# The decayed keys of the HGRN heads: turned by TensorE, or by VectorE blocks and a trip through memory

## The chip, the core and the metric

The kernel runs on one core of a Trainium2 chip. A core has five engines with an instruction stream each: TensorE (PE in the profile, its weight loads PEld), VectorE (DVE), ScalarE (ACT), GpSimd (POOL) and SyncE (SP). Each runs its own stream strictly in order; semaphores hold an instruction back until what it needs has been done elsewhere. The metric is the device time of one execution in microseconds, lower is better.

## The reference, cut to what matters

One layer of a diffusion backbone on 256 latent tokens and 256 context tokens, model width 2048. After a norm, one projection feeds a convolution branch and a bidirectional gated linear recurrence (HGRN) with 8 heads of 128 channels; both are merged, projected, and followed by an MLP. The part in question is the recurrence. For each head, with keys `k = 1 - f` and gates `f` out of a sigmoid:

```python
def hgrn_final_state(k, v, logf):
    a = jnp.cumsum(logf, axis=1)
    return jnp.einsum('blhk,blhv->bhkv', k * jnp.exp(a[:, -1:] - a), v)
...
s_f = hgrn_final_state(kc_f, vc, lfc_f)
s_b = hgrn_final_state(jnp.flip(kc_b, 1), jnp.flip(vc, 1), jnp.flip(lfc_b, 1))
...
o, _, _ = hgrn_bidir(q_prep(p_q), to_heads(p_i.astype(f32)), hgrn_forget(p_ff, lb_f),
                     hgrn_forget(p_fb, lb_b), s_f, s_b)
```

The state of a head is a sum over the 256 context tokens of (decayed key) times (value), in both directions: two matrices of 128 by 128. The latent tokens then read that state and each other.

## The kernel before, in words

Weights stream from memory as tiles of 128x1024 float32, fetched by SP (`fetch`, line 86). `Stream.prepare` splits each into a rounded part `whi` on ACT (line 124) and the rest `wlo` on DVE (line 127); four tiles are kept ready (`AHEAD = 4`). A product is three passes on PE, `mm3` (lines 242 to 247, recorded at line 188): high by high, high by low, low by high.

The heads run in a loop in `run` (lines 781 to 797). Loop step h computes the two gate projections of head h on PE (four weight tiles, 96 matmuls of 128x512), `gates` takes their sigmoid into a page `fg`, and `self.head(h, ...)` is pushed on a list of background generators. `pump` is called after every 12 matmuls: it lets up to three of these generators (`LIVE = 3`) issue a few instructions each. A generator yields a number for the time that it has just issued, which is taken from a budget, or `None`, which means "nothing more from me until the next pump". So a `yield None` puts one pump, 12 matmuls, between a producer and its consumer. What is issued by a pump stands in each engine's stream at that place. `finish` pumps until a generator has ended.

A head (`head`, line 1419) works on `x6`, six blocks of 256 columns with channels on partitions: the keys of the context (blocks 0 and 5), the keys of the latent tokens (1 and 4), the queries (2 and 3). The pool holds two `x6`. In eight levels DVE multiplies decays into them (lines 1466, 1467 and 1469) while ACT copies halves out (`left`, `right`, line 1456) and PE multiplies these into score blocks (lines 1495 and 1502). After the last level, the context keys are decayed but still lie channels by tokens, and the state needs them tokens by channels. This is the turn in question:

- before, four PE transposes into a PSUM bank (line 1522) and one ACT copy of the bank to `kt` (line 1524), then the state on PE (line 1530), its copy on ACT (line 1533), and one pump later the head's output on PE (lines 1539 and 1541), its copy (line 1545) and the count `self.ended += 1` (line 1549).

Elsewhere the kernel has a turn of another kind: the MLP's hidden values are turned in 32x32 blocks by DVE (`turn_blocks`, line 1250), written to a DRAM tile by one DMA of POOL (`swapped`, line 1284) and read back by four (line 1287), so that the DMAs move whole blocks to their places; the consumer waits ten pumps.

In the same stage DVE also runs `dots` (line 1314), sums over modulation weights, one 128x1024 pass a tile.

Of the kernel before, what the change touches and what calls it, by code (L numbers as in the profile page):

```python
# [8 lines left out]
F32 = mybir.dt.float32  # L9
# [6 lines left out]
P = 128  # L16
T = 256
# [120 lines left out]
class Kernel:  # L138
# [247 lines left out]
    def run(self):  # L386
        nc, a = self.nc, self.a
# [208 lines left out]
        def both(k):  # L596

            pg = hp[k].rearrange("p (i s t) -> p s i t", i=2, s=2)
            return pg[:, 0], pg[:, 1]
# [22 lines left out]
        def gates(accs):  # L622

            e = self.page(F32, "fg")
            for d, acc in enumerate(accs):
                o = e[:, 2 * d * T:2 * (d + 1) * T]
                if d:
                    o = bass.AP(o.tensor, o.offset + T, [o.ap[0], [-T, 2], [1, T]])
                    acc = acc.rearrange("p (i t) -> p i t", i=2)
                nc.scalar.activation(out=o, in_=acc, func=AF.Sigmoid)  # L630
            return e
# [148 lines left out]
        heads = []  # L780
        for h in range(NH):
            accs = []
            for d in range(2 * (h > 0)):
                accs.append(self.bank())
                for hf in range(2):
                    hi, lo = st.next()
                    for k8 in range(8):
                        k = 8 * hf + k8
                        s = slice(k8 * P, (k8 + 1) * P)
                        self.mm3(accs[d], (hi[:, s], lo[:, s]), both(k), k == 0, k == KT - 1)  # L790
                        if k8 == 3 or k8 == 7 and (d, hf) != (1, 1):
                            self.pump(1.95)
            e = gates(accs) if h else self.fg0
            heads.append(self.push(self.head(h, e, self.vp[h // 4])))
            if h > 2:
                self.finish(heads[h - 3])
            self.pump(1.95)


# [619 lines left out]
    def head(self, h, e, vp):  # L1419
# [8 lines left out]
        nc = self.nc  # L1428
        ev = e[:, :TW].rearrange("p (i t) -> p i t", t=T)
        for d in range(2):  # L1430
            s = e[:, 2 * d * T:2 * (d + 1) * T]
            nc.vector.tensor_scalar(out=s, in0=s, scalar1=self.lbm[:, 8 * d + h:8 * d + h + 1], scalar2=self.lb[:, 8 * d + h:8 * d + h + 1],
                                    op0=ALU.mult, op1=ALU.add)
        yield 0.7
        x6 = self.sp.tile([P, 6 * T], F32, name="x6", tag="x6", bufs=2)
        nc.scalar.activation(out=x6[:, 0:2 * T], in_=e[:, 0:2 * T], func=AF.Copy, scale=-1.0, bias=1.0)
        nc.scalar.activation(out=x6[:, 4 * T:6 * T], in_=e[:, 2 * T:4 * T], func=AF.Copy, scale=-1.0, bias=1.0)
# [33 lines left out]
        for levels in ((0, 1, 2), (4, 8, 16), (32, 64, 128)):  # L1471
# [18 lines left out]
            for n, (m, left, right) in enumerate(ops):  # L1490
                for b in range(2):
                    for g in range(2):
                        o = b * P + g * 64
                        r = b * P + (1 - g) * 64 if m == 64 else o
                        nc.tensor.matmul(ps[64 * g:64 * g + 64, n * P + b * 64:n * P + b * 64 + 64], left[:, o:o + 64],  # L1495
                                         right[:, r:r + 64] if right is not None else halves(2 * T + o, T, 64, m), start=True, stop=True)
            if levels[-1] == 128:
                far = self.bank()
                for b in range(2):
                    w = x6[:, T:T + P] if b == 0 else x6[:, 4 * T + P:5 * T]  # L1500
                    r = x6[:, 3 * T + P:4 * T] if b == 0 else x6[:, 2 * T:2 * T + P]
                    nc.tensor.matmul(far[:, b * P:(b + 1) * P], w, r, start=True, stop=True)  # L1502
            for n, (m, _, _) in enumerate(ops):
# [6 lines left out]
                else:  # L1510
                    i = LEVELS.index(m)
# [4 lines left out]
                nc.scalar.copy(out=sc4[:, 1:3, :], in_=far[:, :T].rearrange("p (b t) -> p b t", b=2))  # L1516
            decay(levels[-1])
            yield 1.8
        yield None
        pt = self.bank()  # L1520
        for j, o in enumerate((0, P, 5 * T, 5 * T + P)):
            nc.tensor.transpose(out=pt[:, j * P:(j + 1) * P], in_=x6[:, o:o + P], identity=self.v["ident"])
        kt = self.small(512, "kt")
        nc.scalar.copy(out=kt, in_=pt)
        yield None
        c = (h % 4) * P
        ps = self.bank()
# [8 lines left out]
        for tb in range(2):  # L1536
            o = po[:, tb * P:(tb + 1) * P]
# [6 lines left out]
        o = self.at(self.on, h)  # L1544
# [182 lines left out]
```

## Time and profile before

| | |
|---|---|
| time, median of 3 runs | 1625.0 us (1624.18 to 1625.57) |
| the profiled execution | 1623.7 us, span 1621.9 us |
| granted TensorE clock | 0.999 |
| busy share of the span | PE 99%, PEld 82%, DVE 71%, ACT 50%, POOL 3% |
| stage of the heads | about 206 us to 475 us of the span |
| transposes at line 1522 | 32, from 239.0 us to 464.8 us |

Busy times come from one profiled execution, in which times are counted from the span's start. Matmuls are pipelined: the profile gives a 128x512 matmul about 0.39 us, but the next one starts 0.23 us later, so what a matmul costs is read from start to start. A wait shows as idle time before an instruction, with the instruction or DMA that ended it.

### The profile page before, as it was taken

Reading aid. Unit: us, or ns where it says so; the run is one execution under the profiler, and the core shown is the slowest. Engines: PE = TensorE matmul, PEld = TensorE weight load, DVE = VectorE, ACT = ScalarE, POOL = GpSimd, SP = SyncE. Lnnn points to the kernel's source line nnn. Section 1 sums busy time; section 2 is a strip of 40 time slices with the busy share of each in tenths; the row PEclk is TensorE's granted clock in tenths of the full one; section 3 lists DMA queues with packets and bytes.
Section 4 is the critical chain, followed back from the end, with each engine's and each line's share of the span. In section 5 each row is a group of like instructions: output and inputs, shape, how many; then the busy total and the mean of one; then the engine's idle time right before and its main releaser. Section 6 shows DMA issues by size and latency. Waiting matters only on the chain.

```text
span 1621.9 us, 22046 instructions
## 1 busy us (share of the span) xinstructions
PE 1606.9 (99%) x8195; PEld 1322.7 (82%) x8195; DVE 1154.8 (71%) x1678; ACT 804.7 (50%) x1166; POOL 52.2 (3%) x98
## 2 busy tenths in 40 slices
PE   7999999999999999999999999999999999999998
PEld 5768888888888888888888888888888888888887
DVE  5886887787868889967887765555665665655556
ACT  6553454455654444653446665444443454435543
POOL 0000000000000000000000001000110011001000
PEclk9999999999999999999999999999999999999999
DMA  9997954444666556678887378866887688677773
GB/s 378 409 388 269 326 192 140 156 146 141 221 206 212 189 192 205 231 271 299 324 289 266 135 255 263 271 205 224 288 277 246 213 270 270 228 242 239 232 219 116
DMA packets 109148, 391.00 MB, mean 241 GB/s; under 512 B 12912, under 2 KB 13808, under 8 KB 109040
## 3 DMA queue, kind: packets, MB, share of 16 engines
q1 hardware_dynamic: 102096, 368.34, 66.3%
q0 software_dynamic: 6656, 20.99, 4.4%
q8 instruction: 64, 1.05, 0.3%
q14 instruction: 44, 0.36, 0.1%
q10 hardware_dynamic: 288, 0.26, 0.0%
HBM read 379.06 MB, written 10.49 MB: 240 GB/s over the span
## 4 chain that ended last, share of the span: by engine, by line
PE 92%; DMA 5%; DVE 1%; issue 1%; ACT 1%; SPq 0%; ACTq 0%; DVEq 0%
PE bank L188 80%; PE bank L255 5%; PE bank L257 3%; DMA raw<-wi 2%; DMA rawpage<-wm 1%; PE bank L1495 1%; DMA rawpage<-wms 1%; DMA x<-ctx 1%; PE bank L1541 0%; PE bank L1539 0%; PE bank L1530 0%; DVE wlo L127 0%; DMA raw<-wpw 0%; PE bank L1502 0%; ACT whi L124 0%
## 5 line engine op out<-in xcount | busy, mean ns | idle before, releaser
L127 DVE TENSOR_TENSOR wlo<-raw,whi 128x1024 fp32r<-128x1024 f32 x488 | 593.5, 1223 | 335.1 <-ACT whi L124 329.2
L124 ACT ACTIVATE whi<-raw 128x1024 fp32r<-128x1024 f32 x488 | 512.7, 1059 | 592.0 <-PE bank L188 388.2
L188 PE MATMUL bank<-whi,h 128*128 128x512 f32 x2160 | 674.1, 390 | 2.0 <-DVE h L673 1.1
L188 PEld LDWEIGHTS bank<-whi,h 128*128 128x128 f32 x2160 | 405.2, 188 | 87.4 <-DVE h L673 2.0
L188 PE MATMUL bank<-wlo,h 128*128 128x512 f32 x1080 | 420.9, 390 | 1.1 <-DVE wlo L127 1.1
L188 PEld LDWEIGHTS bank<-wlo,h 128*128 128x128 f32 x1080 | 202.8, 188 | 44.7 <-DVE wlo L127 3.0
L188 PE MATMUL bank<-whi,hidh 128*128 128x512 f32 x503 | 195.0, 388 | 0.0
L188 PE MATMUL bank<-wlo,hidh 128*128 128x512 f32 x503 | 195.0, 388 | 0.0
L188 PE MATMUL bank<-whi,hidl 128*128 128x512 f32 x503 | 195.0, 388 | 0.0
L188 PE MATMUL bank<-h,whi 128*128 128x512 f32 x512 | 164.7, 402 | 0.1
L188 PEld LDWEIGHTS bank<-h,whi 128*128 128x128 f32 x512 | 91.8, 188 | 23.4 <-issue 5.8
L188 PEld LDWEIGHTS bank<-wlo,hidh 128*128 128x128 f32 x503 | 94.5, 188 | 19.5
L188 PEld LDWEIGHTS bank<-whi,hidl 128*128 128x128 f32 x503 | 94.5, 188 | 19.3
L188 PEld LDWEIGHTS bank<-whi,hidh 128*128 128x128 f32 x503 | 94.5, 188 | 19.2
L188 PE MATMUL bank<-h,wlo 128*128 128x512 f32 x256 | 100.2, 391 | 0.0
L255 PE MATMUL bank<-h,whi 128*128 128x512 f32 x384 | 97.2, 395 | 0.0
L255 PEld LDWEIGHTS bank<-h,whi 128*128 128x128 f32 x384 | 69.0, 189 | 12.6
L1314 DVE SCALAR_TENSOR_TENSOR raw<-raw,silu_row 128x1024 f32<-128x1024 f32 x64 | 76.8, 1220 | 1.6 <-DMA raw<-wmt 1.5
L1301 DVE SCALAR_TENSOR_TENSOR gacc<-raw,silu_c,gacc 128x1024 f32<-128x1024 f32 x60 | 76.7, 1279 | 0.3 <-DMA raw<-wm 0.3
L188 PEld LDWEIGHTS bank<-h,wlo 128*128 128x128 f32 x256 | 48.0, 188 | 10.1
L257 PEld LDWEIGHTS bank<-h,wlo 128*128 128x128 f32 x384 | 52.4, 190 | 3.8
L257 PE MATMUL bank<-h,wlo 128*128 128x256 f32 x384 | 53.5, 282 | 0.0
(251 smaller groups left out, 1355.0 us busy)
## 6 DMA issues: line engine op xcount, KB each, us to landing
raw<-w SPq DMA_DIRECT2D x256, 512.0 KB, 4.7
raw<-wi SPq DMA_DIRECT2D x172, 512.0 KB, 4.3
raw<-wmt SPq DMA_DIRECT2D x64, 512.0 KB, 4.1
raw<-wm SPq DMA_DIRECT2D x64, 512.0 KB, 4.7
rawpage<-wm SPq DMA_DIRECT2D x42, 512.0 KB, 10.1
raw<-wo SPq DMA_DIRECT2D x32, 512.0 KB, 4.6
raw<-who SPq DMA_DIRECT2D x16, 512.0 KB, 4.9
raw<-wpw SPq DMA_DIRECT2D x16, 512.0 KB, 5.7
```

Of the source, the lines that this page charges most:

```text
L124: kn.his.append(nc.scalar.activation(out=hi, in_=raw, func=AF.Copy))
L127: kn.los.append(nc.vector.tensor_tensor(lo, raw, hi.bitcast(F32), op=ALU.subtract))
L188: ins = fn(*args, **kw)
L255: nc.tensor.matmul(bank, w[0][:, cut(i)], x(k)[2], start=(k == 0), stop=False)
L257: nc.tensor.matmul(bank[:, T:], w[1][:, cut(i)], x(k)[0], start=False, stop=(k == nk - 1))
L1301: nc.vector.scalar_tensor_tensor(acc, raw, s, acc, op0=ALU.mult, op1=ALU.add)
L1314: nc.vector.scalar_tensor_tensor(raw, raw, 1.0, self.srow, op0=ALU.mult, op1=ALU.mult, accum_out=self.dot[:, 32 * j + b:32 * j + b + 1])
L1495: nc.tensor.matmul(ps[64 * g:64 * g + 64, n * P + b * 64:n * P + b * 64 + 64], left[:, o:o + 64], right[:, r:r + 64] if right is not None ...
```

## The change

The four PE transposes, their PSUM bank and the copy out of PSUM go. In their place DVE turns the four 128x128 key blocks in squares of 32x32 (two instructions), the result goes to the first half of the head's own gate page, POOL writes it to a DRAM tile `kthere` with one DMA and reads it back into the second half of that page with four DMAs that move 32 partitions each, and after three more pumps ACT copies it, with blocks reordered, to `kt`. Two orders change with it: a head now waits, pump by pump, until the head two in front of it has ended before it takes its `x6`; and in the loop `finish(heads[h - 3])` stands ahead of the gates of head h instead of behind the push.

```diff
@@ run, loop over heads @@
                         if k8 == 3 or k8 == 7 and (d, hf) != (1, 1):
                             self.pump(1.95)
+            if h > 2:
+                self.finish(heads[h - 3])
             e = gates(accs) if h else self.fg0
             heads.append(self.push(self.head(h, e, self.vp[h // 4])))
-            if h > 2:
-                self.finish(heads[h - 3])
             self.pump(1.95)
@@ head @@
         yield 0.7
+        while self.ended < h - 1:
+            yield None
         x6 = self.sp.tile([P, 6 * T], F32, name="x6", tag="x6", bufs=2)
...
             decay(levels[-1])
             yield 1.8
-        yield None
-        pt = self.bank()
-        for j, o in enumerate((0, P, 5 * T, 5 * T + P)):
-            nc.tensor.transpose(out=pt[:, j * P:(j + 1) * P], in_=x6[:, o:o + P], identity=self.v["ident"])
+        flip, back = e[:, 0:512], e[:, 512:1024]
+        for d, o in enumerate((0, 5 * T)):
+            nc.vector.transpose(out=flip.rearrange("p (j b r) -> p b j r", j=4, b=4)[:, 2 * d:2 * d + 2],
+                                in_=x6[:, o:o + T].rearrange("p (b j r) -> p b j r", b=2, j=4))
+        there = self.dr.tile([P, 512], F32, name="kthere", tag="kthere", bufs=2)
+        nc.gpsimd.dma_start(there, flip)
+        for j in range(4):
+            nc.gpsimd.dma_start(back[32 * j:32 * j + 32].rearrange("c (i f) -> c i f", i=4),
+                                there[:, j * P:(j + 1) * P].rearrange("(i c) f -> c i f", i=4))
+        yield 0.9
+        for _ in range(3):
+            yield None
         kt = self.small(512, "kt")
-        nc.scalar.copy(out=kt, in_=pt)
+        nc.scalar.copy(out=kt.rearrange("p (b i r) -> p b i r", i=4, b=4), in_=back.rearrange("p (i b r) -> p b i r", i=4, b=4))
         yield None
```

What it does to the streams, at head 0 (its keys are `x_2161`; `h_...` are the blocks of the normed tokens that the weights multiply, `x_2430` and `x_2431` is the next head's `x6`). On PE before, from the last score matmuls of the head (line 1502) to the transposes:

```order
L1502 MATMUL bank<-x_2161 128x128 x2
L188 MATMUL bank<-h_370,whi 128x512 x2
L188 MATMUL bank<-h_370,wlo 128x512
L188 MATMUL bank<-h_458,whi 128x512 x2
L188 MATMUL bank<-h_458,wlo 128x512
L188 MATMUL bank<-h_549,whi 128x512 x2
L188 MATMUL bank<-h_549,wlo 128x512
L188 MATMUL bank<-h_612,whi 128x512 x2
L188 MATMUL bank<-h_612,wlo 128x512
L1522 MATMUL bank<-pack,x_2161 128x128 x4
```

On PE now the transposes are gone, and the state's matmuls (line 1540 now) stand further down: in heads 0 to 5, 60 matmuls of 128x512 and the next head's first score matmuls (12 at line 1497) lie between line 1504, which was 1502, and line 1540; before, 24 or 36 of 128x512 lay between 1502 and the state. Around it at head 0:

```order
L188 MATMUL bank<-h_612,whi 128x512 x2
L188 MATMUL bank<-h_612,wlo 128x512
L1540 MATMUL bank<-v_1430,kt 128x128 x4
L188 MATMUL bank<-h_685,whi 128x512 x2
L188 MATMUL bank<-h_685,wlo 128x512
```

On DVE now, the last decays of head 0 (lines 1468 and 1469), the new block turns (line 1523) and what stands around them. Before, the same rows stood there without line 1523, and one of the two `dots` (line 1314) now stands between the decay and the turns:

```order
L1514 COPY_PREDICATED sc<-masks,bank 128x128
L127 TENSOR_TENSOR wlo<-raw,whi 128x1024
L1468 TENSOR_TENSOR x_2161<-x_2161,fg 128x3x128
L1469 TENSOR_TENSOR x_2161<-x_2161,fg 128x3x128
L1314 SCALAR_TENSOR_TENSOR raw,dot<-raw,silu_row 128x1024
L1523 STREAM_TRANSPOSE fg<-x_2161 128x2x4x32 x2
L1314 SCALAR_TENSOR_TENSOR raw,dot<-raw,silu_row 128x1024
```

On ACT before, around the copy of the turned keys of head 0:

```order
L1516 COPY sc<-bank 128x256
L1437 ACTIVATE x_2430<-fg 128x512
L1524 COPY kt<-bank 128x512
L1456 COPY left<-x_2430 128x256
L1456 COPY right<-x_2430 128x256
L124 ACTIVATE whi<-raw 128x1024
L1533 COPY state<-bank 128x256
```

On ACT now, where the copy (line 1534 now) waits for the four DMAs that read back; the split of a weight tile and the next head's copies are queued behind it:

```order
L1508 COPY sc<-bank 128x128
L1458 COPY left<-x_2431 128x256
L1458 COPY right<-x_2431 128x256
L1534 COPY kt<-fg 128x512
L124 ACTIVATE whi<-raw 128x1024
L1458 COPY left<-x_2431 128x256
L1458 COPY right<-x_2431 128x256
L1543 COPY state<-bank 128x256
```

The copy has moved behind several of the next head's copies. POOL, which before issued nothing in the stage of the heads but two memsets (line 812), now has eight times one DMA out and four back there. From the end of the last head to the end of the kernel PE, DVE and ACT keep their order.

## The prediction

> **What bounds the kernel now.** I read the first part of the page, then the waits of PE over the stage of the heads, then that stage cut into stretches, then PE's timeline around one turn.
>
> ```profile
> span 1621.9 us, 22046 instructions
> PE 1606.9 (99%) x8195; PEld 1322.7 (82%) x8195; DVE 1154.8 (71%) x1678; ACT 804.7 (50%) x1166; POOL 52.2 (3%) x98
> PE 92%; DMA 5%; DVE 1%; issue 1%; ACT 1%; SPq 0%; ACTq 0%; DVEq 0%
> core 0: us, PE busy (x) PEld busy (x) DVE busy (x) ACT busy (x) POOL busy (x), PEclk, DMA share, GB/s
> 236.00:267.00 31.00, 31.00 (x204) 25.41 (x202) 24.72 (x48) 15.03 (x35) 0.00 (x0) 1.00 0.42 137
> 301.00:332.00 31.00, 31.00 (x206) 25.78 (x204) 23.23 (x47) 15.08 (x34) 0.00 (x0) 1.00 0.45 148
> 364.50:393.00 28.50, 28.50 (x190) 23.27 (x186) 23.41 (x47) 14.43 (x35) 0.00 (x0) 1.00 0.47 159
> ```
>
> PE is busy in all 31.00 of 31.00 us of such a stretch, the chain that ends last is 92% PE, and the list of PE's waits between 206 and 475 us comes back empty. So time taken from PE's stream in this stage is gained in full, and any idle PE is lost in full. The other engines have room: DVE 23.41 of 28.50, ACT about half, POOL all of it, the DMA engines about half.
>
> **What goes from PE.** PE's timeline at head 0's turn (start, duration, line, count):
>
> ```profile
> 234.74 0.39 PE L188 MATMUL bank<-h,wlo 128*128 128x512 f32 x1
> 235.05 0.69 PE L1495 MATMUL bank<-right,left 128*64 128x64 f32 x16
> 235.67 0.71 PE L1502 MATMUL bank<-x 128*128 128x128 f32 x4
> 236.14 0.71 PE L188 MATMUL bank<-h,whi 128*128 128x512 f32 x2
> ...
> 238.06 0.39 PE L188 MATMUL bank<-h,wlo 128*128 128x512 f32 x1
> 238.29 0.62 PE L188 MATMUL bank<-h,whi 128*128 128x512 f32 x2
> 238.74 0.39 PE L188 MATMUL bank<-h,wlo 128*128 128x512 f32 x1
> 238.97 0.60 PE L1522 MATMUL bank<-pack,x 128*128 128x128 f32 x4
> 239.33 0.71 PE L188 MATMUL bank<-h,whi 128*128 128x512 f32 x2
> 239.88 0.40 PE L188 MATMUL bank<-h,wlo 128*128 128x512 f32 x1
> L1522 PE MATMUL bank<-pack,x x32: 270/272/273, 239.0 to 464.8; 128*128 128x128 f32 x32
> ```
>
> Three matmuls take 0.68 us (238.06 to 238.74), 0.227 each. From the first transpose (238.97) to the third matmul behind the turn (239.88) pass 0.91 us, of which two matmuls are 0.455: the turn costs 0.455 us. There are 32 transposes, 8 turns: **3.6 us off PE**. The PSUM bank gone gives nothing, since nothing waits for one.
>
> **When the turned keys are due.** By the change's order, between line 1504 (now) and the state's matmuls (1540) of heads 0 to 5 stand 60 matmuls, 60 x 0.227 = 13.65 us, and 12 score matmuls, which the trace records as 24: at 0.62 us for 16 (235.05 to 235.67) that is 0.93. With 0.47 for 1504 itself (235.67 to 236.14) PE comes to 1540 **15.1 us** after 1504 began. Heads 6 and 7 have more matmuls there (112 and 96, some of half width) and some 2 to 5 us more room.
>
> **When they are there.** DVE at head 0 before, then the rows of its block turn and of the old copy:
>
> ```profile
> 236.02 1.23 DVE L127 TENSOR_TENSOR wlo<-raw,whi 128x1024 fp32r<-128x1024 f32 x1
> 237.17 0.56 DVE L1466 TENSOR_TENSOR x<-x,fg 128x384 f32<-128x384 f32 x1
> 237.63 0.55 DVE L1467 TENSOR_TENSOR x<-x,fg 128x384 f32<-128x384 f32 x1
> 238.56 1.22 DVE L1314 SCALAR_TENSOR_TENSOR raw<-raw,silu_row 128x1024 f32<-128x1024 f32 x1
> L1250 DVE STREAM_TRANSPOSE turned<-rsq x32: 704/711/712, 958.1 to 1530.0; 128x512 f32<-128x512 f32 x32
> L1524 ACT COPY kt<-bank x8: 568/587/590, 239.6 to 465.1; 128x512 f32<-128x512 f32 x8
> ```
>
> The last decay ends 2.5 us after 1502 began (235.67 to 238.18). In heads 0, 3, 4 and 5 the change puts one pass of `dots` between it and the turns, 1.2 us. A turn of 256 columns isn't in the trace; 512 columns take 0.71, so two take 0.7 to 1.4 by bounds, and I take 0.8, near the lower since most of it goes by columns. So the blocks are turned at 2.5 + 1.2 + 0.8 = 4.5 us. In head 1 only a decay of 0.55 comes between and in both heads 1 and 2 no weight split comes before: some 1.2 to 1.7 us earlier.
>
> Then the trip. Its nearest rows are the MLP's, of twice the bytes: POOL's timeline of one page of hidden values, with the times from issue to landing of its DMA out and of its four back, then of all 64 back, then writes of the size in question on another queue.
>
> ```profile
> 1349.44 0.56 POOL L1284 DMA_DIRECT2D there<-turned  x1 [25.06 <-DVE turned L1250]
> 1352.88 2.19 POOL L1287 DMA_DIRECT2D back<-there  x4 [2.88 <-ACT relu L1023]
> DMA to landing us min/median/max: 2.9/2.9/2.9
> DMA to landing us min/median/max: 4.4/6.6/7.4
> DMA to landing us min/median/max: 3.8/6.6/9.0
> out<-xr SPq DMA_DIRECT2D x5, 256.0 KB, 2.8
> ```
>
> 512 KB out land after 2.9, 256 KB on SP's queue after 2.8; I take 2.8 (2.5 to 2.9). POOL issues the way back 3.44 after the way out, 0.5 after its landing. Four issues take 2.19, so the last is issued 1.64 after the first. It lands, at 128 KB, 7.4 after its issue in this page; the fastest of all 64 needed 3.8, the slowest 9.0. Half the bytes, in pieces of 512 B rather than 1 KB, lie between: 3.8 if only the fixed part counts, 7.4 if the number of pieces, which is the same, sets it. I take the middle, 5.6. The trip is 2.8 + 0.5 + 1.64 + 5.6 = 10.5 us, with bounds of 8.4 and 12.4. ACT's copy adds 0.6 (0.587; its source in SBUF with blocks reordered is taken as no slower). Together 4.5 + 10.5 + 0.6 = **15.6 us**.
>
> [...]
>
> **The sum.** 15.6 against 15.1: PE waits about 0.5 us at the state in heads 0, 3, 4 and 5 and not in the others, 2.0 us. -3.6 + 2.0 = -1.6 us on the profiled execution's 1623.7, 1622.1. The median of the runs lies 1.3 above that execution, so 1623.4.
>
> **What else is touched, and what hides it.** DVE gets 0.8 us a head more; it is idle for 5 to 8 us in each stretch above, and `wlo` is three tiles, 3 x 24 x 0.227 = 16 us, ahead. Without that cover it would cost 8 x 0.8 = 6.4. ACT waits at `kt` for the landing, up to some 4 us a head; behind it stand a weight split, with the same 16 us of cover, the next head's `left` and `right`, whose PE consumers stand at or behind 1540 and wait with it, and `state`, due one pump (2.7 us) after 1540. Uncovered, that would be 4 x 8 = 32 us. SP's queue isn't passed by anything. POOL's two memsets for the convolution now stand behind the seventh head's DMAs; they are needed only after the heads. The two order edits are put at 0:
>
> ```profile
> L1436 ACT ACTIVATE x<-fg x8: 612/630/635, 208.7 to 407.9; 128x512 f32<-128x512 f32 x8
>   PE bank L1539: 6.9, 4
> L1562 DVE SCALAR_TENSOR_TENSOR o<-o,osq,silu_g x16: 344/348/354, 648.1 to 700.0; 128x128 f32<-128x128 f32 x16
> ```
>
> ACT already waited at the new `x6` for the output matmuls of the head two in front (6.9 us in 4 heads), because there are two `x6`; the wait only moves from ACT's stream into the order of issue. The last head ends later, but its first reader comes at 648 us. Were that cover gone, the 6.9 us would be the price.
>
> **The rivals.**
>
> *The trip is hidden wholly* (chance 0.36). If the landing shrinks with the bytes, to under some 5.0, the sum is under 15.1 and only the gain is left: 1623.7 - 3.6 + 1.3 = 1621.4. For it: DMA share 0.42 to 0.47 here, and the heads' DMAs follow nothing on their queue. Against it: even 128 KB with nothing before it needed 7.4.
>
> *The trip is late everywhere, and slower* (0.24). If the number of pieces sets the landing, the trip is 12.4, the keys come at 17.5, 2.4 late in four heads, and about 1.2 and 0.7 late in heads 1 and 2: 11.5 us lost, 11.5 - 3.6 = 7.9, so 1632.9. The place is the first matmul of line 1540. It decides from 1.7 us late in four heads, where the loss is 6.9 and the sum passes +3.25. For it: the piece count stays. Against it: the stage's lower DMA load. [...]
>
> *POOL is held by DVE* (0.04). [...]
>
> **How the numbers follow.** The forecast, a trip that fits or misses by a few tenths, has 0.36 and 1623.4, its own range 1621.8 to 1628.2. A run of this kernel can tell 0.2%, 3.25 us: faster is below 1621.75, slower above 1628.25. The hidden trip counts as faster, 0.36; the forecast and the held POOL as the same, 0.40; the late trip as slower, 0.24. The range reaches from 1620.8, the whole gain and the 0.6 by which runs differ, to 1633, the late trip; beyond it lie only landings above 7.4, and what is not foreseen.
>
> **What would show it.** In the changed kernel's trace: no line 1522; PE's gain of 0.455 us a head; the last of the four DMAs back landing 5.6 us after issue and 10.5 after the DMA out was issued; idle time of PE before line 1540, ended by `kt`, of about 0.5 us in four heads and none in heads 6 and 7; ACT idle before `kt`, ended by a DMA. Wrong would be the forecast if PE idles at lines 1497 or 188 (then ACT or DVE carries the wait on), or if a landing is above 7 or below 4.5.

## The result and the profile after

The changed kernel takes 1621.9 us at the median (1620.6 to 1624.0), the kernel before 1624.9 on the same chip (1623.5 to 1625.8). The ratio is 0.9983 with a 95% interval of 0.9977 to 0.9988: 3.0 us faster (1.9 to 3.7), a gain that the interval keeps clear of zero, though a little less than the 0.2% that the prediction took as its bound. The forecast was 1623.4, the rival with the hidden trip 1621.4. The time lies beside the rival; it is inside the forecast's own range, 1621.8 to 1628.2, by only 0.1 us.

The page of the changed kernel, whose profiled execution took 1622.9 us:

```profile
span 1620.8 us, 22095 instructions
PE 1603.9 (99%) x8163; PEld 1321.3 (82%) x8163; DVE 1160.9 (72%) x1694; ACT 803.8 (50%) x1166; POOL 74.0 (5%) x138
PE 94%; DMA 2%; DVE 2%; ACT 1%; issue 1%; SPq 0%; ACTq 0%; DVEq 0%
```

PE has 32 instructions and 3.0 us less. DVE has 6.1 us more, POOL 21.8. The span alone is only 1.1 us shorter, which is less than the medians say. Where that comes from can be seen at two weight tiles, the 37th and the 113th that ACT splits: one as the stage begins, one 66 us behind its end. First before, then after (start, duration, line):

```profile
203.92 1.06 ACT L124 ACTIVATE whi<-raw 128x1024 fp32r<-128x1024 f32 x1 [2.02 <-DMA raw<-wi]
542.30 1.06 ACT L124 ACTIVATE whi<-raw 128x1024 fp32r<-128x1024 f32 x1 [1.66 <-PE bank L188]
```
```profile
206.52 1.06 ACT L124 ACTIVATE whi<-raw 128x1024 fp32r<-128x1024 f32 x1 [2.03 <-DMA raw<-wi]
540.88 1.06 ACT L124 ACTIVATE whi<-raw 128x1024 fp32r<-128x1024 f32 x1 [1.66 <-PE bank L188]
```

Between the two tiles lie 338.38 us before and 334.36 after: the stage gained 4.0 us. What comes ahead of it, the loading at the start that the change doesn't touch, took 2.6 us longer in this one execution. In all profiles below, this start differs from the one before by -1.1 to +2.6 us, whatever the edit; so single profiles are compared by the stage between these two tiles, and kernels by their medians.

The stage in the same three stretches as before, then as a whole:

```profile
core 0: us, PE busy (x) PEld busy (x) DVE busy (x) ACT busy (x) POOL busy (x), PEclk, DMA share, GB/s
236.00:267.00 31.00, 31.00 (x202) 25.42 (x201) 24.09 (x50) 15.46 (x35) 2.87 (x5) 1.00 0.50 168
301.00:332.00 31.00, 31.00 (x203) 25.73 (x202) 25.57 (x52) 13.95 (x33) 2.73 (x5) 1.00 0.55 177
364.50:393.00 28.50, 28.50 (x192) 23.68 (x191) 24.18 (x50) 14.66 (x35) 2.74 (x5) 1.00 0.53 175
206.00:475.00 269.00, 268.74 (x1784) 226.16 (x1783) 219.08 (x417) 141.09 (x297) 23.43 (x42) 1.00 0.57 188
```

And what PE waited for between 206 and 490 us:

```profile
engine line waited for: us in total, times, longest us
PE bank L1549 <- ACT state L1543: 0.3, 1, 0.3
```

PE is busy all through the three stretches as before. Of 269 us it idles 0.26, once, for `state` in head 6, and not for the turned keys.

The new instructions, each line with its count, its shortest, median and longest time in ns, and the start of the first and last:

```profile
L1523 DVE STREAM_TRANSPOSE fg<-x x16: 401/422/446, 241.8 to 463.0; 128x256 f32<-128x256 f32 x16
L1526 POOL DMA_DIRECT2D kthere<-fg x8: 561/561/692, 242.9 to 463.7; - x8
DMA to landing us min/median/max: 2.3/3.5/4.6
L1528 POOL DMA_DIRECT2D fg<-kthere x32: 548/551/556, 247.9 to 469.0; - x32
DMA to landing us min/median/max: 2.2/3.6/6.9
L1534 ACT COPY kt<-fg x8: 608/622/622, 252.2 to 475.6; 128x512 f32<-128x512 f32 x8
  DMA fg<-kthere: 14.1, 4
L1540 PE MATMUL bank<-v,kt x64: 270/275/275, 253.9 to 478.2; 128*128 128x128 f32 x64
```

The row under line 1534 is ACT's own idle time at the copy: 14.1 us in four heads, and PE waits for none of these copies. Head 0 as an example, on PE, DVE, POOL and ACT:

```profile
238.27 0.71 PE L1504 MATMUL bank<-x 128*128 128x128 f32 x4
241.84 0.77 DVE L1523 STREAM_TRANSPOSE fg<-x 128x256 f32<-128x256 f32 x2
242.92 0.69 POOL L1526 DMA_DIRECT2D kthere<-fg  x1 [242.48 <-DVE fg L1523]
247.89 2.18 POOL L1528 DMA_DIRECT2D fg<-kthere  x4 [4.27 <-DMA kthere<-fg]
252.19 0.62 ACT L1534 COPY kt<-fg 128x512 f32<-128x512 f32 x1 [0.58 <-DMA fg<-kthere]
253.91 1.05 PE L1540 MATMUL bank<-v,kt 128*128 128x128 f32 x8
```

Counted from the start of line 1504, the blocks are turned at 4.3 us, the copy ends at 14.6 and PE arrives at 15.6. All eight heads, worked out from the same rows of the trace (us after the start of line 1504; the trip runs from the issue of the DMA out to the last landing back):

| head | blocks turned | out lands after | trip | last back lands after its issue | copy ends | PE at line 1540 |
|---|---|---|---|---|---|---|
| 0 | 4.3 | 4.3 | 9.2 | 2.6 | 14.6 | 15.6 |
| 1 | 4.8 | 2.3 | 8.6 | 4.0 | 14.4 | 15.3 |
| 2 | 2.7 | 2.3 | 10.1 | 5.5 | 13.9 | 15.3 |
| 3 | 4.3 | 4.3 | 9.2 | 2.7 | 14.6 | 15.3 |
| 4 | 4.3 | 4.6 | 9.4 | 2.7 | 14.7 | 15.3 |
| 5 | 4.3 | 3.2 | 8.2 | 2.8 | 14.6 | 15.3 |
| 6 | 5.7 | 3.8 | 12.1 | 6.2 | 18.9 | 21.2 |
| 7 | 3.3 | 3.1 | 11.8 | 6.5 | 16.1 | 17.3 |

The keys are ready 0.6 to 1.4 us before PE in heads 0 to 5. That is a thin margin, and the experiments ask how thin.

### The profile page after: what moved, and what is told of

Its sections match the earlier page's. It is cut to its first block, busy times and chain, and to the rows that moved or that the text cites. A ratio compares the mean times of both kernels' runs of the same rounds, so it can differ in the third digit from the quotient of the medians.

```text
span 1620.8 us, 22095 instructions
## 1 busy us (share of the span) xinstructions
PE 1603.9 (99%) x8163; PEld 1321.3 (82%) x8163; DVE 1160.9 (72%) x1694; ACT 803.8 (50%) x1166; POOL 74.0 (5%) x138
## 3 DMA queue, kind: packets, MB, share of 16 engines
q8 instruction: 64, 1.05, 0.3%
## 4 chain that ended last, share of the span: by engine, by line
PE 94%; DMA 2%; DVE 2%; ACT 1%; issue 1%; SPq 0%; ACTq 0%; DVEq 0%
PE bank L188 83%; PE bank L255 5%; PE bank L257 2%; PE bank L1497 1%; DMA raw<-wi 1%; DVE wlo L127 1%; DMA x<-x 0%; DMA raw<-wpw 0%; PE bank L1549 0%; PE bank L1551 0%; ACT whi L124 0%; PE bank L1540 0%; DMA fg<-kthere 0%; PE bank L1504 0%; PE bank L1360 0%
## 5 line engine op out<-in xcount | busy, mean ns | idle before, releaser
L188 PEld LDWEIGHTS bank<-h,whi 128*128 128x128 f32 x512 | 92.5, 188 | 23.9 <-issue 5.8
```

What stands on the lines that cost most here:

```text
L188: ins = fn(*args, **kw)
```

## The experiments

The theory after the result: the gain is PE's four transposes a head and nothing else; the trip costs nothing because it ends about one us before PE comes; every us beyond that is lost in full. The rivals: the gain comes from the two order edits; or the trip still costs part of the gain somewhere; or the time from memory is so safe that the pumps could be fewer. Ratios are against the kernel before on the same chip. "Stage" is the change of the time between the two tiles above, in one profile each; for the changed kernel it is -4.0.

**The transposes put back, with nobody reading them.** Four PE transposes into a bank, one pump after the block turns; all the rest as changed:

```diff
         yield 0.9
-        for _ in range(3):
+        yield None
+        pt = self.bank()
+        for j, o in enumerate((0, P, 5 * T, 5 * T + P)):
+            nc.tensor.transpose(out=pt[:, j * P:(j + 1) * P], in_=x6[:, o:o + P], identity=self.v["ident"])
+        for _ in range(2):
             yield None
```

> The changed kernel with the four PE transposes of each head put back one pump after the block turns, into a bank that nothing reads. If the gain is PE time taken out of a stream that never waits, they cost 8 x 0.455 = 3.6 us and the kernel is back near 1625.5 us, level with the kernel before. If the gain came from the two order edits, or from merged groups, it stays near 1622 us.

Measured: 1624.9 us, ratio 1.000 (0.9992 to 1.0009), stage +0.6. The whole gain is gone. It was PE's time for the transposes; trip, block turns and order edits together neither add nor cost anything beyond the interval, 1.4 us to either side.

**The order edits alone.** The kernel before, with its transposes, and with `finish` moved and the wait for the head two in front:

```diff
+            if h > 2:
+                self.finish(heads[h - 3])
             e = gates(accs) if h else self.fg0
             heads.append(self.push(self.head(h, e, self.vp[h // 4])))
-            if h > 2:
-                self.finish(heads[h - 3])
...
+        while self.ended < h - 1:
+            yield None
         x6 = self.sp.tile([P, 6 * T], F32, name="x6", tag="x6", bufs=2)
```

> The kernel before with the two order edits alone: a head waits for the end of the one two in front, and that finish stands ahead of the gates; the PE transposes stay. If the edits are worth nothing, 1624.9 us, same as before within 0.7 us. If they carry part of the gain, 1622 to 1624 us.

Measured: 1624.2 us, ratio 0.9997 (0.9988 to 1.0006), stage +0.4. The list of PE's waits in the stage stays empty. The order edits by themselves change nothing that this run can tell, as the prediction had put them.

**No trip.** The five DMAs are left out and the copy reads the turned blocks where DVE put them, so the 32x32 blocks stay at wrong places and the state isn't the reference's; the work on PE, DVE and ACT is the same:

```diff
-        there = self.dr.tile([P, 512], F32, name="kthere", tag="kthere", bufs=2)
-        nc.gpsimd.dma_start(there, flip)
-        for j in range(4):
-            nc.gpsimd.dma_start(back[32 * j:32 * j + 32].rearrange("c (i f) -> c i f", i=4),
-                                there[:, j * P:(j + 1) * P].rearrange("(i c) f -> c i f", i=4))
...
-        nc.scalar.copy(out=kt.rearrange("p (b i r) -> p b i r", i=4, b=4), in_=back.rearrange("p (i b r) -> p b i r", i=4, b=4))
+        nc.scalar.copy(out=kt.rearrange("p (b i r) -> p b i r", i=4, b=4), in_=flip.rearrange("p (i b r) -> p b i r", i=4, b=4))
```

> The changed kernel without the five DMAs of each head: the copy reads the block turns directly, so that blocks stay in their old places and the state is not the reference's. It shows what the trip costs while it is hidden. If it is wholly hidden and the added traffic (512 KB a head) disturbs nothing, 1621.9 us within 0.7 us. If the trip still costs PE something (a late state in heads 6 and 7, weight tiles that come later), 0.5 to 2 us faster.

Measured: 1622.1 us, ratio 0.9984 (0.9975 to 0.9992), stage -4.0, the same as with the trip. Hidden as it is, the trip costs nothing that can be told here: neither by its wait nor by what its bytes take from the weights' DMAs.

**One pump fewer for the trip.** PE then comes 12 matmuls, 2.7 us, earlier:

```diff
         yield 0.9
-        for _ in range(3):
+        for _ in range(2):
             yield None
         kt = self.small(512, "kt")
```

> The changed kernel with two pumps instead of three between the trip and the copy of the keys. The state's matmuls are then due 12 x 0.227 = 2.7 us earlier, 12.6 us after line 1504 begins instead of 15.3. In the changed kernel's trace the copy ends 13.9 to 14.7 us after it in heads 0 to 5. If the trip really fits by only 0.6 to 1.4 us, PE then waits 1.3 to 2.1 us in each of six heads (11.2 us in all) and about 1.5 us in head 7: 1633 to 1636 us, with PE idle before line 1540. If something else gives way (a trip that shortens, or engines that run further ahead than the trace shows), it stays below 1625 us.

Measured: 1634.5 us, ratio 1.0062 (1.0048 to 1.0076), stage +11.4. PE's waits between 206 and 830 us:

```profile
engine line waited for: us in total, times, longest us
PE bank L1540 <- ACT kt L1534: 9.7, 5, 2.9
PE bank L188 <- DVE wlo L127: 1.1, 2, 1.0
```

And PE's windows around the waits of head 2 (the first two rows) and head 3:

```profile
core 0: us, PE busy (x) PEld busy (x) DVE busy (x) ACT busy (x) POOL busy (x), PEclk, DMA share, GB/s
313.70:317.11 3.41, 1.67 (x9) 1.09 (x8) 1.49 (x3) 0.94 (x3) 0.00 (x0) 1.00 0.84 268
317.11:320.53 3.42, 3.42 (x20) 2.95 (x20) 1.31 (x3) 1.07 (x3) 0.00 (x0) 1.00 0.15 61
347.84:351.25 3.41, 1.39 (x10) 1.35 (x11) 2.89 (x6) 2.11 (x4) 0.00 (x0) 1.00 0.10 23
351.25:354.66 3.41, 3.41 (x10) 2.64 (x9) 1.93 (x4) 0.48 (x2) 0.00 (x0) 0.50 0.79 282
354.66:358.08 3.42, 3.42 (x44) 3.10 (x44) 0.73 (x2) 1.35 (x4) 0.00 (x0) 1.00 0.45 162
```

Five heads of eight wait (1.9, 1.7, 2.1, 1.1 and 2.9 us in heads 0, 2, 3, 6 and 7); the other three were in time, though not by their trips of 7.5 to 8.3 us alone: in heads 4 and 5 the blocks were turned 0.9 and 1.7 us earlier than in the changed kernel, and in head 1 five more matmuls stand ahead of line 1540 in this program's order, so that PE came there 13.8 us after line 1504 and not 12.6. The third pump is needed: it is what separates 3 us of gain from 9.8 us of loss. The windows show something that no theory had asked for: after the wait of head 3 the granted clock of PE (column PEclk) goes to 0.50 for 3.4 us and comes back; after the wait of head 2 it stays at 1.00. The longer trip, below, shows it more plainly. So the time lies in the expected range partly by luck: the waits at line 1540 came to 9.7 us and not 11.2, and the clock, which the expectation didn't have, added to them. Over the six executions the time goes with the clock, from 1630.8 us at a mean of 0.999 to 1640.3 at 0.996.

**One pump more.** `range(4)` at the same place.

> The changed kernel with four pumps. If the trip is hidden already with three, nothing is gained: 1621.9 us within 1 us. If unprofiled executions lose time to late landings, up to 1 us is gained. If the longer chain of a head costs something by itself, slower.

Measured: 1623.3 us, ratio 0.9990 (0.9981 to 0.9998), stage -2.6. No gain from more room, and none was to be had, since PE waits only 0.3 us in the changed kernel's stage. Between 206 and 830 us PE now waits 1.4 us for `wlo` and 0.8 for `left` at line 1497. The interval overlaps that of the changed kernel, so it isn't shown that it is slower.

**A longer trip.** A second hop through memory, DRAM to DRAM, before the way back:

```diff
         nc.gpsimd.dma_start(there, flip)
+        first, there = there, self.dr.tile([P, 512], F32, name="kagain", tag="kagain", bufs=2)
+        nc.gpsimd.dma_start(there, first)
```

> The changed kernel with a second hop between two DRAM tiles in the trip, nothing else moved. The hop adds its landing, 2.3 to 4.5 us by the rows of the way out, and 0.5 us until the next issue: 2.8 to 5 us. The trip of 8.2 to 10.1 us fits by about 1 us in heads 0 to 5 and by 2.3 and 1.2 in heads 6 and 7, so PE should wait 2 to 4 us in six heads and 1 to 4 in the others: 14 to 30 us, 1636 to 1652 us. If ScalarE or VectorE buffer the delay instead, it stays within 3 us of the changed kernel.

Measured: 1644.9 us, ratio 1.0127 (1.0112 to 1.0143), stage +20.2, with trips of 10.5 to 17.4 us. More than the hop moved: in the order of this program the state's matmuls stand 3 or 4 matmuls further down in heads 0, 3, 4 and 5 and 7 in head 1. PE's waits between 206 and 830 us:

```profile
PE bank L1542 <- ACT kt L1536: 16.3, 6, 4.7
PE bank L188 <- DVE wlo L127: 0.8, 1, 0.8
```

PE's timeline at the stall of head 0, then the windows there:

```profile
252.73 0.39 PE L188 MATMUL bank<-h,wlo 128*128 128x512 f32 x1
256.00 2.08 PE L1542 MATMUL bank<-v,kt 128*128 128x128 f32 x8 [2.89 <-ACT kt L1536]
257.74 1.20 PE L188 MATMUL bank<-h,whi 128*128 128x512 f32 x2
258.74 0.55 PE L188 MATMUL bank<-h,wlo 128*128 128x512 f32 x1
```
```profile
core 0: us, PE busy (x) PEld busy (x) DVE busy (x) ACT busy (x) POOL busy (x), PEclk, DMA share, GB/s
255.00:256.00 1.00, 0.00 (x0) 0.00 (x0) 0.96 (x3) 0.62 (x1) 0.00 (x0) 0.82 0.95 283
256.00:257.00 1.00, 0.99 (x4) 1.00 (x5) 0.10 (x1) 0.00 (x0) 0.00 (x0) 0.50 0.89 307
257.00:258.00 1.00, 1.00 (x7) 1.00 (x6) 0.00 (x0) 0.00 (x0) 0.00 (x0) 0.50 0.84 332
258.00:259.00 1.00, 1.00 (x4) 0.81 (x4) 0.00 (x0) 0.68 (x2) 0.00 (x0) 0.50 0.72 295
259.00:260.00 1.00, 1.00 (x5) 0.81 (x5) 0.00 (x0) 0.00 (x0) 0.00 (x0) 0.97 0.07 29
```

This is the rival "late everywhere" made real. The state's matmuls (eight records) take 2.08 us there instead of 1.05, at half the clock. The waits named are 17.1 us, but the time is 20.5 us above the kernel before, and so 23.5 above the changed one. The clock about closes the gap: the missing shares of the windows at head 0 add to 0.18 + 3 x 0.50 + 0.03 = 1.71 us of full clock, and the same drop comes at three more of the stalls; 17.1 + 4 x 1.7 = 23.9. With one pump fewer it came twice: 9.7 + 1.1 + 2 x 1.7 = 14.2 by this reckoning, 9.8 + 3.0 = 12.8 by the medians, 15.4 by the stage of the profile.

**The same turn for the readout.** Line 1577, behind the heads, has 16 more PE transposes: the heads' outputs, two a head. DVE turns them here in blocks, two heads at a time, with the same five DMAs; the copies follow six pumps later:

```diff
-            ps = self.bank()
-            for tb in range(2):
-                nc.tensor.transpose(out=ps[:, tb * P:(tb + 1) * P], in_=o[:, tb * P:(tb + 1) * P], identity=self.v["ident"])
...
+            nc.vector.transpose(out=flip.rearrange("p (j b r) -> p b j r", j=4, b=4), in_=pair.rearrange("p (b j r) -> p b j r", b=4, j=4))
+            there = self.dr.tile([P, 512], F32, name="kthere", tag="kthere", bufs=2)
+            nc.gpsimd.dma_start(there, flip)
+            for i in range(4):
+                nc.gpsimd.dma_start(pair[32 * i:32 * i + 32].rearrange("c (i f) -> c i f", i=4),
+                                    there[:, i * P:(i + 1) * P].rearrange("(i c) f -> c i f", i=4))
...
+        for _ in range(6):
+            yield None
```

> The changed kernel with the readout's 16 PE transposes (line 1577) turned the same way: per pair of heads one VectorE block turn of 512 columns, one DMA out and four back, and the copies with gains six pumps later. 16 x 0.112 = 1.8 us leave PE; the readouts run in the background 50 us ahead of their reader. If PE time in an unbroken stream is what counts, 1620.1 us. If VectorE, which is fuller there, or the end of the readouts becomes the bound, 1622 us or slower.

Measured: 1626.1 us, ratio 1.0009 (1.0000 to 1.0017). That is some 4 us slower than the changed kernel, where a gain was hoped for. PE's longest wait is for a weight split:

```profile
PE bank L188 <- ACT whi L124: 4.0, 1, 4.0
```

ACT's timeline shows what that split stood behind:

```profile
666.07 1.06 ACT L124 ACTIVATE whi<-raw 128x1024 fp32r<-128x1024 f32 x1 [0.57 <-DMA raw<-wi]
674.67 0.91 ACT L1594 ACTIVATE turned<-o,pack 128x256 f32<-128x256 f32 x2 [7.53 <-DMA o<-kthere]
675.48 0.70 ACT L240 ACTIVATE h<-turned 128x256 fp32r<-128x256 f32 x2
676.09 1.04 ACT L124 ACTIVATE whi<-raw 128x1024 fp32r<-128x1024 f32 x1
```

The copy waits 7.5 us for its DMA. The next `whi` is queued behind it on ACT, and that costs PE 4.0 us. Then the clock falls here too, and for twice as long as in the heads, 6.82 us against 3.41 (columns as above):

```profile
674.38:677.80 3.42, 0.49 (x1) 0.19 (x1) 0.64 (x1) 3.12 (x6) 2.27 (x5) 1.00 0.86 335
677.80:684.62 6.82, 6.18 (x15) 4.82 (x16) 6.79 (x6) 5.86 (x10) 2.10 (x4) 0.50 0.81 249
684.62:688.04 3.42, 3.42 (x17) 2.81 (x16) 0.07 (x1) 3.23 (x6) 0.00 (x0) 1.00 0.20 78
```

At half the clock, 6.8 us cost up to 3.4 more. With a wait of 0.8 us for `wlo` behind it that is up to 8.2 us, and 6.4 with the 1.8 of the transposes taken off, where the medians show some 4: this sum isn't closed. The 50 us of room that was expected wasn't there: `finish` needs the readout at this point and issues the rest of it without matmuls between, so the six pumps were no distance at all.

**The readout's turn put ahead of the convolution,** and as its control **that order alone,** with the PE transposes kept. Both put the two readouts at the head of the list of generators:

```diff
-        for j in range(2):
-            heads.append(self.push(self.readout(j)))
+        for j in reversed(range(2)):
+            gen = self.readout(j)
+            self.bg.appendleft(gen)
+            heads.append(gen)
```

> The readout turned by the trip as in e7, with the readouts put ahead of the convolution in the list of background generators, so that the copies no longer queue on ScalarE just ahead of the next stage's weight splits. In e7 ScalarE idled 7.5 us before a readout copy, ended by a DMA, and PE idled 4.0 us for whi. If that place was all that was wrong, the 16 transposes' 1.8 us are gained: 1620.1 us, PE without such a wait between 540 and 700 us. If the readout's trip costs in itself, 1622 us or slower.

> The changed kernel with the readouts ahead of the convolution and nothing else, the PE transposes of the readout kept: the control for e8. If only PE time counts, as the changed kernel, 1621.9 us within 0.7 us, and 1.8 us above e8.

The changed kernel was run once more beside them:

> The changed kernel itself, on the same chip as e8 and e9, for comparison: 1621.9 us within 0.7 us.

Measured: with the turn 1622.7 us, ratio 0.9988 (0.9979 to 0.9996); the order alone 1622.9, 0.9992 (0.9983 to 1.0001); the changed kernel 1622.4, 0.9981 (0.9972 to 0.9990). PE's waits between 540 and 720 us, where the readouts run, with the turn, then with the order alone:

```profile
PE bank L188 <- DVE wlo L127: 2.6, 5, 0.7
```
```profile
PE bank L188 <- DVE wlo L127: 0.9, 2, 0.5
```

The trip is hidden now, as PE waits for no copy, and the clock stays at 1.00. But `wlo` is late there, by 2.6 us with the turn and 0.9 with the order alone; the changed kernel has no such wait in this stretch. The 16 transposes are worth at most 16 x 0.114 = 1.8 us by the price of the heads' turn, and the 1.7 us of further waits take about as much. So the 1.8 us between the two runs that was expected is not there: they can't be told apart, and neither beats the changed kernel. None of the other runs does either. Why DVE is late with the turn wasn't tested.

## Why the prediction was right, and where it was off

**PE's gain, 0.455 us a head, 3.6 us.** Right. The time came to -3.0 us with 1.9 to 3.7 by the interval; putting the transposes back takes all of it away. The stage of the profiles shows 4.0 to 4.3. The 0.4 to 0.7 beyond the 3.6 isn't explained: PE's short score matmuls lie in fewer separate groups now, which might save that, but no run tested it.

**When the keys are due, 15.1 us.** Right: 15.3 in five heads and 15.6 in head 0. Heads 6 and 7 had 6.1 and 2.2 us more, where 2 to 5 were said, and their trips of 12.1 and 11.8 needed it.

**Blocks turned at 4.5 us.** Right: 4.3 in heads 0, 3, 4 and 5 (0.77 us for the two instructions, 0.8 taken). The 4.8 of head 1 is 1.5 to 2 us later than said, and was covered by a trip of 8.6.

**The trip, 10.5 us with bounds of 8.4 and 12.4.** This is the step that failed, by its size: 8.2 to 9.4 us in heads 0, 1, 3, 4 and 5 and 10.1 in head 2, where the blocks were 1.6 us earlier. Two of its terms were off in opposite directions. The way out was taken as 2.8 (2.5 to 2.9) and took 2.3 to 4.6. The last landing back was taken as 5.6, midway between the two MLP rows, and took 2.6 to 2.8 in four heads, less than the 3.8 that was its lower bound; only heads 2, 6 and 7 were near or above 5.6. So the "0.5 late in four heads" came out as 0.6 to 1.4 us early in all six, and the 2.0 us of loss in the sum was none. The condition of the rival with the hidden trip, a last landing under some 5.0, held in five of these six heads, and its 1621.4 is 0.5 from the time. So the path was right, but the wait that the forecast priced did not occur: that the time still lies at the lower end of the forecast's own range is luck, and the mechanism that the runs show is the rival's.

The choice of the middle was the mistake. The 7.4 was one page's DMA of twice the bytes, in another stage; 3.8, the fastest of 64, was nearer to the case in hand, and even that was no bound from below.

**What was put at nothing.** DVE's extra 0.8 us a head is hidden in the idle time that was named (6.1 us more busy time, no wait on DVE). ACT's wait for the landing is 14.1 us in all, up to 5.9 in head 7, and passes on at most the 0.3 us for `state` in head 6 (in the second profile of the changed kernel it was 13.0 us, and PE waited for nothing); the cover is the weight tiles ahead, as said. It is real cover, and not a rule: in the readout, without it, the same copy's wait of 7.5 us cost PE 4.0 and the clock after it. The order edits at 0 fit the run with them alone.

**The late trip.** It wasn't this kernel, but two runs were made into it. The mechanism was as described: PE idles at the state's first matmul, and nothing catches it up. Its price was too low. The sum counted each us of wait once, 7.9 us beyond the kernel before for 2.4 us late in four heads; the clock took 1.7 us more after each of six waits of 2.1 to 4.7 us in these runs, which for four heads makes, as an estimate, 4 x 1.7 = 6.8 us more.

**POOL held by DVE.** No run shows it. Of 40 issues of POOL in the changed kernel's stage, 39 took 0.55 to 0.56 us, and the longest, at head 0, 0.69.

## What to carry to other kernels

Where TensorE never idles, take small work off it even if the way round is some twenty times as long (8 to 12 us for 0.455), but count the distance in matmuls between the issue and the consumer, and measure how thin the margin is: here one pump of 2.7 us fewer turns 3 us of gain into 9.8 of loss. The distance must be one that the order of issue keeps: a generator that is finished on the spot gives none. And look at what is queued behind the waiting copy on its own engine, since that decides whether its wait is free (14.1 us at no cost in the heads) or not (7.5 us for 4.0 and a fall of the clock to 0.50 in the readout).

## What the runs showed of the hardware

**After seven waits of TensorE the granted clock fell to 0.50 and came back to 1.00.** Four were with the longer trip, two with one pump fewer, one in the readout. Six times it was half the clock for 3.41 us, a loss of 1.7 us of full clock; in the readout it lasted 6.82 us. The seven waits were of 2.1 to 4.7 us; five others in the two runs with late keys, of 0.7 and 1.1 us with the longer trip and of 1.1, 1.7 and 1.9 us with one pump fewer, had no fall behind them. The fall came 2.5 to 4.6 us after PE stopped, even where PE had gone on by then: at head 3 with one pump fewer PE resumed at 349.86 and the clock fell at 351.25. What decides whether it falls, and why it lasted twice as long in the readout, is open: no run varied either by itself.

**DMA landings by POOL's queue scatter.** The same 256 KB out landed after 2.3 us in heads 1 and 2, after 4.3 to 4.6 in heads 0, 3 and 4, and after 3.1 to 3.8 in the others. In heads 0, 3 and 4, where it was late, the last way back was quick (2.6 to 2.7 us), so that the trip hardly changed. The reason is open: no run varied it.
